# A new order of the mixer steps in a two-layer diffusion backbone, and modulation weights loaded in rows of 2 KB

## The chip, the cores and the metric

The kernel runs on one core of a Trainium2 chip. Its time is device microseconds of one execution; the median of three runs of the kernel before is 1035.23 us (1034.37 to 1036.27). The core has a tensor engine (PE in the rows, with its weight loads as PEld), a vector engine (DVE), a scalar engine (ACT), GpSimd (POOL) and SyncE (SP), which here issues most of the DMA transfers. Each engine works through its own list of instructions in order and waits where one of them needs another engine's result. The clock granted to PE has two levels here, 1.2 and 2.4 GHz; the profile shows it as PEclk, 0.5 and 1.0.

## The reference, cut to what matters

One inference step through two layers. 128 context tokens and 256 latent tokens, width 1024. Each layer modulates a normalised input by six vectors that come from a conditioning vector and a weight matrix (w_ada, 1024 x 6144), runs a token mixer and then a SwiGLU channel mixer:

```python
def adaln(cvec, w, b):
    mod = jnp.einsum('nd,de->ne', jax.nn.silu(cvec), w) + b
    return jnp.split(mod[:, None, :], 6, axis=-1)

def trunk_layer(x, mods, mixer_w, g_norm_l, w_gu_l, w_down_l, ctx):
    sh1, sc1, ga1, sh2, sc2, ga2 = mods
    h = modulate(rms_norm(x, g_norm_l[0]), sh1, sc1)
    mix, new_ctx = token_mixers(h, *mixer_w, ctx)
    x = x + ga1 * rms_norm(mix, g_norm_l[1])
    f = swiglu(modulate(rms_norm(x, g_norm_l[2]), sh2, sc2), w_gu_l, w_down_l)
    x = x + ga2 * rms_norm(f, g_norm_l[3])
    return x, new_ctx
```

The token mixer projects its input once (w_in), feeds three parallel groups of heads, and projects their joined outputs (w_out). A is neighbourhood attention with a relative bias (4 heads), B grouped-query attention with normalised and rotated queries and keys (8 query heads, 2 key heads), C a bidirectional mLSTM in chunks of 64 (4 heads), with gates, a running maximum, weighted scores, states from a cache and an output gate:

```python
    z = jnp.einsum('btd,de->bte', h, w_in_l)
    ...
    h_ml, fin_f, fin_b = mlstm_bidir(mq, mk, mv, mg, st_f0, st_b0)
    o_ml = mlstm_output(h_ml, mo, g_ml_l)
    mix = jnp.concatenate([merge_heads(o_na), merge_heads(o_gqa), o_ml], axis=-1)
    out = jnp.einsum('bte,ed->btd', mix, w_out_l)
```

All is float32. A product with weights is made of three matmuls on a high and a low part of each operand.

## The kernel before, in words

All 384 tokens stay in SBUF as three blocks of 128. A layer is a mixer, then a channel mixer (ffn). Weights stream from HBM by SP into the raw buffers (tag raw, three slots; line 126). Each is split into a high part by ACT (line 118) and a low part by DVE (line 119), and three matmuls use them (lines 108 to 110).

Inside a mixer the order of work on PE, DVE and ACT is written by hand: SCHEDULE holds one string of tokens for each layer, and step() runs them one after the other (line 1192 on). Each token's instructions join the lists of the three engines in that order; POOL and SP are not bound by it, and take their work as the framework orders it. The tokens that matter here:

- f: the next piece of projection work (71 in a layer): the input projection, first to the gates, then to tiles named tps (transposed results) or fps (features of queries and keys), later the first part of the output projection. A1 to A4 bring on the splits of weights ahead.
- t (layer 0 only): one of 12 chunks of 1 MB of w_ada, loaded into araw (two slots, line 167) and multiplied on PE (adap, line 219), added on DVE (acc, line 227). When a vector is complete, PE turns it (adat, line 237) and DVE makes Bmod (line 244), or it is spread over all partitions by POOL into G (line 210). In the channel mixer the other chunks are multiplied on DVE (line 177).
- s: the next small job of the norm and rotation of queries and keys.
- scans and rexp: the mLSTM's gates, with four kinds of scans on DVE (lines 800 to 813).
- L, E, C, U with a number 0 to 3: one unit of the mLSTM, a pair of heads in one direction. L loads the weights' rows into W by POOL (line 865) and masks them (line 868); E takes exponentials on ACT (line 885); C multiplies them by the scores S on DVE (line 909, or 894 and 895; units 0 and 2 also compute S on PE, line 907, for the unit that follows); U sums on PE (nd, lines 920 and 924) and divides on DVE (lines 929 to 939). W2 takes the buffer of the key weights kw, free after cout, and W3 that of W0, free after U0. S of the second pair takes the PSUM banks of the first.
- krow, kw, cin, cout, decay, cols: key weights (line 961), states in and out (line 968), decays.
- ogate: the output gate, two passes on ACT (lines 976 and 977) and a multiplication on DVE (line 978).
- hsum, hrstd, hnorm: the norm of the mLSTM's heads (line 1001 frees hml).
- bias, K0, K1: SP loads the relative bias, nb, in eight transfers (line 1088), the second four into the buffer that hml used; K0 and K1 transpose the cached keys on PE and mask the bias on DVE (line 1092).
- rT, rmix, kout: the mLSTM's outputs turned and joined; keys to the output.
- c, e, p, v with a number: one unit of attention: scores on PE (sc, line 1019), soft-max on ACT and DVE (nm, P, line 1033), its transposes (ptp, line 1048) and the products with the values.
- b, r, g, x, q, y and digits: the second part of the output projection, the norms and the residual.

The loop that runs the tokens is

```python
        for c in SCHEDULE[l].split():
            step(c)
```

Of the kernel before, what the change touches and what calls it, by code (L numbers as in the profile page):

```python
# [16 lines left out]
D = 1024  # L17
# [3 lines left out]
NEG = -1e30  # L21
SCHEDULE = (
    (
# [9 lines left out]
    ),  # L33
    (
# [8 lines left out]
    ),  # L43
)
ENGINES = {mybir.EngineType.PE, mybir.EngineType.DVE, mybir.EngineType.Activation}
# [7 lines left out]
def hybrid_step(  # L53
# [8 lines left out]
    V, A, PE, G, SP = nc.vector, nc.scalar, nc.tensor, nc.gpsimd, nc.sync  # L62
# [75 lines left out]
    def rstd_from(dst, ss, scale):  # L138
        A.activation(dst, ss, AF.Ln, bias=eps, scale=scale)
        A.activation(dst, dst, AF.Exp, scale=-0.5)  # L140

    Gt = {}

    class Ada:
# [14 lines left out]
        def issue(self, l, vec, kk):  # L159
            e0 = vec * D  # L160
            if kk == 0 and vec in (2, 5):
                for n, src in enumerate((b_ada[l, e0:e0 + D], g_norm[l, vec // 3 * 2 + 1])):
                    for r in range(4):
                        half = r // 2 * 512
                        G.dma_start(gbn[r:128:32, n], src[half:half + 512].rearrange("(g f) -> g f", g=4))
            raw = ap_.tile([128, 2, D], F32, tag="araw", name="araw", bufs=2)
            SP.dma_start(raw, w_ada[l, kk * 256:(kk + 1) * 256, e0:e0 + D].rearrange("(k p) f -> p k f", p=128))
            self.pend += [(l, vec, kk, raw, part) for part in range(self.parts)]

        def mul_v(self, l, vec, kk, raw, part):  # L170
# [35 lines left out]
        def spread(self):  # L206

            for l, n, row in self.rows:
                Gt[l, n] = ap_.tile([128, 2, D], F32, tag="G", name="G", bufs=1)
                G.dma_start(Gt[l, n], row.rearrange("s g f -> s (g f)").unsqueeze(0).broadcast_to([128, 2, D]))  # L210
            self.rows = []

        def mul_p(self, l, vec, kk, raw, part):
# [107 lines left out]
    def half_sum(n, h, ss):  # L321
# [4 lines left out]
        else:  # L326
            A.activation(ss[:, 0:1], ss[:, 1:2], AF.Ln, bias=ss[:, 2:3])
            A.activation(ss[:, 0:1], ss[:, 0:1], AF.Exp, scale=-0.5)

    HALVES = (slice(0, 512), slice(512, 1024))  # L330

    def post(i, halves, dst, g):
        rs = sumsq_rstd(halves)
        for n, h in enumerate(halves):
            V.tensor_tensor(dst[:, HALVES[n]], h, g[:, min(i, 1), HALVES[n]], ALU.mult)
        for h in HALVES:
            V.scalar_tensor_tensor(x[:, i, h], dst[:, h], rs, x[:, i, h], ALU.mult, ALU.add)

    def norm_x(i, t=None):
        rs = sumsq_rstd([x[:, i]])  # L340
        if t is None:
            t = tp.tile([128, D], F32, tag="t4", name="xn")
        for h in HALVES:
            V.tensor_scalar(t[:, h], x[:, i, h], rs, None, ALU.mult)
# [26 lines left out]
    def mixers(l, ma, mp, mn, pp, banks, h1T, steps, pairs, tails):  # L371
# [4 lines left out]
        def out_parts(ch, half):  # L376
            cs = HALVES[half]
            if ch in (0, 3):
                return w_parts(wl_out, 768 if ch == 0 else 0, 2, half * 512, 512)
            j0 = 2 * (ch - 1)  # L380

            def parts(raw):
                rv = raw.rearrange("p (k f) -> p k f", k=2)
                return [(rv[64 * w:64 * w + 64],
                         wl_out[256 + 256 * w + 64 * j0:256 + 256 * w + 64 * (j0 + 2), cs].rearrange(
                             "(j p) f -> p j f", p=64)) for w in range(2)]
            return parts
# [354 lines left out]
        def out_first():  # L742
            ps, w = {}, {}
            for half, ch, i in [(0, 0, i) for i in range(3)] + [
# [6 lines left out]
                if ch:  # L751
                    if not half:
                        oP.append(ma.tile([128, D], F32, tag="m4", name="oP", bufs=4))
                    A.activation(oP[i][:, HALVES[half]], ps[half, i], AF.Copy)
                yield

        def out_second(i):
            ps = [pp.tile([128, 512], F32, tag="w", name="ops2") for _ in range(2)]
            for ch in (1, 2):
                for half, h in enumerate(HALVES):  # L760
                    if i == 0:
# [644 lines left out]
    for l in range(DEPTH):  # L1406
        with tc.tile_pool(name="ma", bufs=1, reuse_waits="tile") as ma, \
                tc.tile_pool(name="mb", bufs=1, reuse_waits="tile") as mb, \
                tc.tile_pool(name="mn", bufs=1, reuse_waits="tile") as mn, \
                tc.tile_pool(name="p_w", bufs=1, space=PSUM, reuse_waits="tile") as p_w, \  # L1410
                ExitStack() as banks:
            pp = Pools({"w": p_w}, {"w": 3})
            pp.single(banks, 5)
            if l == 0:
                h1T, pairs, tails = new_hT(), [], []
            steps = [] if l else [(l, v) for v in (3, 2, 4)]
            if l == 0:
                cp1, cp2 = (pp.tile([128, 512], F32, tag="b", name=n) for n in ("cT", "cT2"))
                with tc.manual_schedule(engines={mybir.EngineType.PE}):
                    PE.transpose(cp1[:, 0:16], crow, ident[0:16, 0:16])  # L1420
                    PE.transpose(cp2[:, 64:128], grow, ident[0:64, 0:64])
                    PE.transpose(cp2[:, 128:224], brow, ident[0:96, 0:96])
                V.tensor_copy(scol[:, :, 2:4], cp1[:, 0:16].rearrange("p (s k) -> p k s", s=2))
                V.tensor_copy(gcol, cp2[:, 64:128].rearrange("p (l n k) -> p l n k", l=DEPTH, n=4))
                V.tensor_copy(bcol, cp2[:, 128:224].rearrange("p (l n k) -> p l n k", l=DEPTH, n=6))
            else:
                spread()
            h2 = mixers(l, ma, mb, mn, pp, banks, h1T, steps, pairs, tails)
# [65 lines left out]
```

## Time and profile before

| of the profiled execution | |
|---|---|
| its time | 1036.46 us |
| its span in the trace | 1034.7 us |
| PE busy | 971.1 us (94%) |
| DVE busy | 622.4 us (60%) |
| ACT busy | 466.3 us (45%) |
| POOL busy | 79.9 us (8%) |
| mean granted clock of PE | 0.969 |
| DMA | 167.21 MB, mean 162 GB/s |

The span runs from the first to the last instruction on the chip; the time holds 1.8 us more around it. Layer 0's mixer reaches to about 255 us and its channel mixer from there to about 523; layer 1's mixer lies from about 560 to 757, and its channel mixer behind it. A share of busy time is a mean over stages: in the channel mixers PE is never idle, and what idle time there is lies in the mixers. In rows of the timeline, the bracket at the end gives the time that the engine stood idle ahead of the instruction and the engine and line that ended it.

### The profile page before, as it was taken

The numbers are of one execution on the slowest core, as the hardware profiler recorded it, in microseconds if no ns is written. First come the engines' busy times: TensorE is split into PE (matmuls) and PEld (weight loads), VectorE is DVE, ScalarE is ACT, GpSimd is POOL, SyncE is SP. The second block draws the span as 40 slices with busy tenths as digits, with TensorE's granted clock in tenths as the row PEclk, the third lists the DMA queues.
The fourth block names the chain that finished last, engine by engine and source line by source line (L and its number), as shares of the span: only waits on it lengthen the run. The fifth ranks groups of instructions, "written<-read, shape, count | busy, mean of one in ns | idle before, by whom it ended". The sixth has DMA issues, their size and how long they took to land.

```text
span 1034.7 us, 15985 instructions
## 1 busy us (share of the span) xinstructions
PE 971.1 (94%) x6375; PEld 854.8 (83%) x6375; DVE 622.4 (60%) x940; ACT 466.3 (45%) x920; POOL 79.9 (8%) x138
## 2 busy tenths in 40 slices
PE   5999689799999999999999996989999999999997
PEld 3879587467999999999988785956699999999996
DVE  3557536567893798977556664476778533333324
ACT  3535514558833333333266454367883333333322
POOL 0302402000000200000210213000000001000000
PEclk9999869899999999999999997899999999999999
DMA  9958728611975587783334453331197434433001
GB/s 325 319 175 234 214 69 256 176 62 53 318 268 177 198 293 244 261 284 125 103 93 140 136 148 93 82 90 60 43 316 243 131 123 150 136 122 122 21 1 62
DMA packets 117052, 167.21 MB, mean 162 GB/s; under 512 B 14961, under 2 KB 89473, under 8 KB 116465
## 3 DMA queue, kind: packets, MB, share of 16 engines
q1 hardware_dynamic: 111328, 153.93, 46.6%
q0 software_dynamic: 5280, 12.10, 4.0%
q8 instruction: 50, 0.82, 0.3%
q14 instruction: 26, 0.21, 0.1%
q10 hardware_dynamic: 368, 0.16, 0.1%
HBM read 163.46 MB, written 2.70 MB: 161 GB/s over the span
## 4 chain that ended last, share of the span: by engine, by line
PE 72%; DVE 6%; ACT 5%; issue 3%; DMA 2%; POOL 0%; SPq 0%; DVEq 0%; ACTq 0%; POOLq 0%
PE gups L110 11%; PE gups L109 11%; PE gups L108 11%; PE facc L108 6%; PE facc L110 6%; PE facc L109 6%; ACT P L1033 2%; PE nd L924 2%; PE ptp L1048 1%; PE sc L1019 1%; PE tps L109 1%; PE tps L110 1%; PE tps L108 1%; PE ops L108 1%; DMA raw<-in_w_out_dram 1%
## 5 line engine op out<-in xcount | busy, mean ns | idle before, releaser
L119 DVE TENSOR_TENSOR lo<-raw,hi 128x1024 fp32r<-128x1024 f32 (+2 forms) x100 | 120.4, 1210 | 85.1 <-ACT hi L118 84.8
L118 ACT ACTIVATE hi<-raw 128x1024 fp32r<-128x1024 f32 (+2 forms) x100 | 103.7, 1042 | 106.8 <-PE facc L110 81.6
L110 PE MATMUL gups<-hT,ring 128*128 128x384 f32 x416 | 140.7, 338 | 0.0
L108 PE MATMUL gups<-hT,ring 128*128 128x384 f32 x416 | 140.7, 338 | 0.0
L109 PE MATMUL gups<-hT,ring 128*128 128x384 f32 x416 | 140.6, 338 | 0.0
L177 DVE SCALAR_TENSOR_TENSOR spare<-araw,scol,spare 128x1024 f32<-128x1024 f32 x98 | 120.7, 1277 | 2.3 <-DMA araw<-in_w_ada_dram 2.0
L108 PE MATMUL facc<-hi,f 128*128 128x512 f32 x240 | 95.6, 398 | 0.0
L109 PE MATMUL facc<-lo,f 128*128 128x512 f32 x240 | 94.7, 395 | 0.0
L110 PE MATMUL facc<-hi,f 128*128 128x512 f32 x240 | 94.7, 395 | 0.0
L109 PEld LDWEIGHTS gups<-hT,ring 128*128 128x128 f32 x416 | 78.2, 188 | 0.5
L108 PEld LDWEIGHTS gups<-hT,ring 128*128 128x128 f32 x416 | 78.1, 188 | 0.5
L110 PEld LDWEIGHTS gups<-hT,ring 128*128 128x128 f32 x416 | 78.1, 188 | 0.0
L108 PE MATMUL gups<-hT,xring 128*128 128x384 f32 x224 | 75.8, 338 | 0.0
L110 PE MATMUL gups<-hT,xring 128*128 128x384 f32 x224 | 75.8, 338 | 0.0
L109 PE MATMUL gups<-hT,xring 128*128 128x384 f32 x224 | 75.7, 338 | 0.0
L108 PE MATMUL tps<-hi,hT 128*128 128x512 f32 (+2 forms) x192 | 67.1, 349 | 2.2 <-DVE hT L509 2.2
L109 PE MATMUL tps<-lo,hT 128*128 128x512 f32 (+2 forms) x192 | 65.3, 340 | 3.4 <-DVE lo L119 3.4
L110 PE MATMUL tps<-hi,hT 128*128 128x512 f32 (+2 forms) x192 | 65.4, 341 | 0.0
L1226 ACT ACTIVATE ring<-rgu 128x1024 fp32r<-128x1024 f32 x26 | 27.6, 1062 | 68.2 <-PE gups L109 35.0
L1226 ACT ACTIVATE ring<-spare 128x1024 fp32r<-128x1024 f32 x26 | 27.5, 1059 | 62.4 <-PE gups L109 37.5
L108 PEld LDWEIGHTS facc<-hi,f 128*128 128x128 f32 x240 | 45.2, 188 | 10.8 <-issue 1.4
L110 PEld LDWEIGHTS facc<-hi,f 128*128 128x128 f32 x240 | 45.2, 188 | 10.5
(299 smaller groups left out, 1995.8 us busy)
## 6 DMA issues: line engine op xcount, KB each, us to landing
araw<-in_w_ada_dram SPq DMA_DIRECT2D x40, 1024.0 KB, 5.6
raw<-in_w_down_dram SPq DMA_DIRECT2D x44, 512.0 KB, 4.7
spare<-in_w_gu_dram SPq DMA_DIRECT2D x20, 1024.0 KB, 5.5
rgu<-in_w_gu_dram SPq DMA_DIRECT2D x20, 1024.0 KB, 5.1
raw<-in_w_in_dram SPq DMA_DIRECT2D x36, 512.0 KB, 5.2
sraw<-in_w_ada_dram SPq DMA_DIRECT2D x16, 512.0 KB, 9.3
raw<-in_w_out_dram SPq DMA_DIRECT2D x8, 512.0 KB, 5.9
raw<-in_w_out_dram SPq DMA_DIRECT2D x16, 256.0 KB, 5.2
```

Of the source, the lines that this page charges most:

```text
L108: PE.matmul(out, lhsT=wh, rhs=xh, start=start, stop=False)
L109: PE.matmul(out, lhsT=wh, rhs=xl, start=False, stop=False)
L110: PE.matmul(out, lhsT=wl, rhs=xh, start=False, stop=stop)
L118: a = A.activation(hi[:, :n], raw, AF.Copy)
L119: v = V.tensor_tensor(lo[:, :n], raw, hi[:, :n].bitcast(F32), ALU.subtract)
L177: V.scalar_tensor_tensor(acc[s], raw[:, part], scol[:, k, 2 + s:3 + s], acc[s], ALU.mult, ALU.add)
L924: PE.matmul(ndv[:, ti, hd], lhsT=W[:, hd, o:o + 128], rhs=vml[:, st, 2 * j + hd], start=ti == 0, stop=ti == 0 or (hd == 1 and n == len(ter ...
L1019: PE.matmul(sc[cc:cc + 64, hd, u * nk:(u + 1) * nk], lhsT=qT[pr, cc:cc + 64], rhs=kT[pr], start=True, stop=True)
L1033: A.activation(Pv[:, hd, u], self.sv[:, hd, u], AF.Exp, bias=nm[:, 0, hd, u:u + 1], accum_out=nm[:, 1, hd, u:u + 1])
L1048: PE.transpose(pt[:, hd, b * 128:(b + 1) * 128], self.P[:, hd, b * 128:(b + 1) * 128], ident)
L1226: A.activation(hi, rv, AF.Copy)
```

## The change

Both strings of SCHEDULE are written in a new order, with the same tokens. The w_ada chunk of 1 MB and the spread of G are each issued as two transfers of 512 KB, one for each half of the columns, so that a row of the w_ada transfer has 2 KB in place of 4 KB. The diff, with one line of each string:

```diff
@@ SCHEDULE, layer 0, the first line of the string
-        "f f f f f f f f f gates scans f f f t f f f f f f f t f s f s rexp L0 s f s f f f s f f Q0 s f s f f f s "
...
+        "f f f f f f f f f f f gates f f t f f f f f f f f scans s s rexp f f s L0 f s f t f f f f f f s Q0 f s "
...
@@ SCHEDULE, layer 1, where units 0 to 2 stand
-        "f s Q1 f s f f Q2 f f f krow f s cols kw decay cin L1 f f E0 C0 s cout L2 E1 s ogate C1 f f U0 L3 s s s "
...
+        "f s f Q1 s f f Q2 f f f krow f cols decay kw f cin E0 L1 f cout C0 L2 s ogate L3 s E1 f C1 s s E2 U0 s "
...
@@ class Ada
+    HALVES = (slice(0, 512), slice(512, 1024))
...
             raw = ap_.tile([128, 2, D], F32, tag="araw", name="araw", bufs=2)
-            SP.dma_start(raw, w_ada[l, kk * 256:(kk + 1) * 256, e0:e0 + D].rearrange("(k p) f -> p k f", p=128))
+            for h in HALVES:
+                SP.dma_start(raw[:, :, h], w_ada[l, kk * 256:(kk + 1) * 256, e0 + h.start:e0 + h.stop].rearrange(
+                    "(k p) f -> p k f", p=128))
...
                 Gt[l, n] = ap_.tile([128, 2, D], F32, tag="G", name="G", bufs=1)
-                G.dma_start(Gt[l, n], row.rearrange("s g f -> s (g f)").unsqueeze(0).broadcast_to([128, 2, D]))
+                for n2, h in enumerate(HALVES):
+                    G.dma_start(Gt[l, n][:, :, h], row[:, 4 * n2:4 * n2 + 4].rearrange("s g f -> s (g f)").unsqueeze(0)
+                                .broadcast_to([128, 2, 512]))
```

The rows below show the lists of single engines at three places, before and then after; lines of the changed kernel are one to four higher or lower than those of the kernel before.

First place: DVE in layer 0, from the gates (gt) to the scans (R). Before:

```order
L712 TENSOR_TENSOR gt<-tps,bg 128x2x4 x6
L783 SCALAR_TENSOR_TENSOR R<-R_707 64x384
L786 SCALAR_TENSOR_TENSOR R_707<-R_707,R 64x384
L800 SCALAR_TENSOR_TENSOR R<-ones,R_707 32x128
L800 SCALAR_TENSOR_TENSOR R<-ones,R_707 32x256
```

And after:

```order
L714 TENSOR_TENSOR gt<-tps,bg 128x2x4 x6
L118 TENSOR_TENSOR lo<-raw,hi 128x1024
L785 SCALAR_TENSOR_TENSOR R<-R_728 64x384
L788 SCALAR_TENSOR_TENSOR R_728<-R_728,R 64x384
L118 TENSOR_TENSOR lo<-raw,hi 128x1024 x3
L802 SCALAR_TENSOR_TENSOR R<-ones,R_728 32x128
L802 SCALAR_TENSOR_TENSOR R<-ones,R_728 32x256
```

Four splits of weights (lo), which stood behind the scans, now stand ahead of them, one ahead of the gates' sums and three behind these.

Second place: PE in layer 0, from the scores of the second pair of heads through units 1 and 2 (nd; a unit is five rows of nd, and two units that meet share a row). Before:

```order
L907 MATMUL S_1375<-qTm,kTm 64x128 x4
L237 MATMUL adat<-cst,acc 128x128
L219 MATMUL adap<-araw,scol 32x128 x16
L924 MATMUL nd<-share,W 128x65 x2
L920 MATMUL nd<-CT,decq 128x130
L924 MATMUL nd<-share,W 128x65 x4
L920 MATMUL nd<-CT,decq 128x130
L924 MATMUL nd<-share,W 128x65 x4
L920 MATMUL nd<-CT,decq 128x130
L924 MATMUL nd<-share,W 128x65 x2
L920 MATMUL nd<-CT,decq 128x130
L924 MATMUL nd<-share,W 128x65 x4
```

And after, from the last projection matmuls between units 1 and 2 to the first behind unit 2:

```order
L108 MATMUL tps<-lo,hT_125 128x256
L109 MATMUL tps<-hi,hT_126 128x256
L241 MATMUL adat<-cst,acc 128x128
L223 MATMUL adap<-araw,scol 32x128 x16
L926 MATMUL nd<-share,W 128x65 x2
L922 MATMUL nd<-CT,decq 128x130
L926 MATMUL nd<-share,W 128x65 x2
L922 MATMUL nd<-CT,decq 128x130
L926 MATMUL nd<-share,W 128x65 x4
L107 MATMUL fps<-hT_125,hi 128x384
L108 MATMUL fps<-hT_126,hi 128x384
L109 MATMUL fps<-hT_125,lo 128x384
```

Before, units 1 and 2 followed each other and adat and adap came ahead of unit 1; now unit 1 follows the scores at once, twelve matmuls of projection (tps), adat and adap come between the two units, and twelve more of projection (fps) between units 2 and 3.

Third place: ACT in layer 1, from the state output (Cout) to the exponentials of the second unit (W), with the two passes of the output gate (share). Before:

```order
L970 ACTIVATE Cout<-cop 65x512
L885 ACTIVATE W<-W,share 128x128 x2
L885 ACTIVATE W<-W,share 128x256
L885 ACTIVATE W<-W,share 128x128 x2
L885 ACTIVATE W<-W,share 128x256
L139 ACTIVATE s_5786<-s_5786,eps 128x2
L140 ACTIVATE s_5786<-s_5786 128x2
L976 ACTIVATE share<-share,ones 128x768
L977 ACTIVATE share<-share 128x768
```

And after:

```order
L972 ACTIVATE Cout<-cop 65x512
L640 ACTIVATE t_5838<-z 128x128
L978 ACTIVATE share<-share,ones 128x768
L979 ACTIVATE share<-share 128x768
L138 ACTIVATE s_5840<-s_5840,eps 128x2
L139 ACTIVATE s_5840<-s_5840 128x2
L887 ACTIVATE W<-W,share 128x128 x2
L887 ACTIVATE W<-W,share 128x256
L887 ACTIVATE W<-W,share 128x128 x2
L887 ACTIVATE W<-W,share 128x256
```

The output gate's two passes now stand ahead of the second unit's exponentials, where they stood behind them.

## Rows read from the trace of the kernel before

**Rows 1.** Table of stretches: start:end, length, busy us (count) by engine, PEclk, DMA share, GB/s

```profile
108.86:147.10 38.24, 27.52 (x236) 24.95 (x236) 16.13 (x44) 11.36 (x31) 9.55 (x14) 0.64 0.38 122
168.90:197.75 28.85, 22.36 (x230) 15.09 (x230) 18.85 (x29) 15.76 (x45) 1.36 (x2) 1.00 0.97 255
255.00:523.00 268.00, 268.00 (x1601) 249.37 (x1600) 206.67 (x224) 106.27 (x147) 13.75 (x25) 1.00 0.66 224
613.88:655.70 41.82, 30.52 (x224) 28.53 (x224) 21.18 (x49) 15.21 (x44) 10.55 (x14) 0.71 0.35 94
638.70:642.10 3.40, 2.33 (x22) 2.33 (x21) 2.36 (x7) 0.84 (x4) 0.00 (x0) 1.00 0.00 0
642.10:655.70 13.60, 10.63 (x41) 10.05 (x40) 7.14 (x18) 3.72 (x8) 0.00 (x0) 0.50 0.12 39
```

**Rows 2.** Timeline, PE: start, us, engine, line, [idle before <- what ended it]

```profile
67.88 0.50 PE L109 MATMUL tps<-lo,hT 128*128 128x512 f32 x1 [1.68 <-DVE lo L119]
...
106.55 1.06 PE L968 MATMUL cop<-kw,share 128*65 128x128 f32 x8 [1.50 <-DVE kw L961]
...
582.81 0.50 PE L109 MATMUL tps<-lo,hT 128*128 128x512 f32 x1 [1.68 <-DVE lo L119]
```

**Rows 3.** Timeline, PE, layer 0, mLSTM units

```profile
112.95 0.63 PE L924 MATMUL nd<-share,W 128*128 128x65 f32 x4 [0.46 <-issue]
...
114.37 1.00 PE L924 MATMUL nd<-share,W 128*128 128x65 f32 x8
118.15 1.32 PE L907 MATMUL S<-qTm,kTm 64*64 64x128 f32 x32 [2.78 <-DVE W L894]
...
123.36 1.94 PE L219 MATMUL adap<-araw,scol 128*32 128x128 f32 x32 [2.66 <-DVE Bmod L244]
```

**Rows 4.** Timeline, layer 0, DVE and then ACT around the second unit

```profile
116.27 0.96 DVE L978 TENSOR_TENSOR share<-share,gml 128x768 f32<-128x768 f32 x1 [1.08 <-ACT share L977]
117.14 0.95 DVE L894 TENSOR_TENSOR W<-W,S 128x768 f32<-128x768 f32 x1
118.01 0.41 DVE L895 TENSOR_TENSOR W<-W,S 128x256 f32<-128x256 f32 x1
...
122.72 2.08 ACT L885 ACTIVATE W<-W,share 128x128 f32<-128x128 f32 x6 [1.85 <-POOL W L868]
```

**Rows 5.** Timeline, layer 1, DVE and then PE, mLSTM units

```profile
628.46 0.96 DVE L978 TENSOR_TENSOR share<-share,gml 128x768 f32<-128x768 f32 x1 [6.53 <-ACT share L977]
...
631.85 1.08 PE L924 MATMUL nd<-share,W 128*128 128x65 f32 x4 [6.54 <-DVE hml L935]
...
639.77 0.66 PE L924 MATMUL nd<-share,W 128*128 128x65 f32 x4 [1.07 <-DVE W L909]
```

**Rows 6.** Timeline, bias tiles: SP's loads, DVE's masks, layers 0 and 1

```profile
157.35 2.61 SPq L1088 DMA_DIRECT2D nb<-in_na_bias_dram  x4
...
169.02 0.56 DVE L1092 TENSOR_TENSOR nb<-nb,cst 128x384 f32<-128x384 f32 x1 [2.79 <-DMA nb<-in_na_bias_dram]
...
661.88 2.61 SPq L1088 DMA_DIRECT2D nb<-in_na_bias_dram  x4
...
670.29 0.56 DVE L1092 TENSOR_TENSOR nb<-nb,cst 128x384 f32<-128x384 f32 x1 [0.75 <-DMA nb<-in_na_bias_dram]
```

**Rows 7.** Timeline, PE and ACT: scores behind soft-max

```profile
200.06 1.56 PE L1019 MATMUL sc<-kTn,qTn 64*64 64x384 f32 x8 [6.80 <-ACT P L1033]
...
197.83 1.06 ACT L118 ACTIVATE hi<-raw 128x1024 fp32r<-128x1024 f32 x1 [6.28 <-DMA raw<-in_w_out_dram]
...
674.54 1.10 PE L1019 MATMUL sc<-share 64*64 64x128 f32 x32 [1.24 <-ACT P L1033]
```

**Rows 8.** DMA issues: what, queue, count, KB each, median us to landing

```profile
araw<-in_w_ada_dram SPq DMA_DIRECT2D x40, 1024.0 KB, 5.6
raw<-in_w_down_dram SPq DMA_DIRECT2D x44, 512.0 KB, 4.7
...
rgu<-in_w_gu_dram SPq DMA_DIRECT2D x20, 1024.0 KB, 5.1
```

More of the change, by code (lines that the diff above doesn't have):

```diff
@@ L328, in half_sum @@
             A.activation(ss[:, 0:1], ss[:, 0:1], AF.Exp, scale=-0.5)
-    HALVES = (slice(0, 512), slice(512, 1024))
     def post(i, halves, dst, g):
```

30 rows, old and new, of the table SCHEDULE are left out of this document.

## The prediction, made before the changed kernel ran

> **What bounds the kernel now.** I read the page's slices first, then the table of stretches, then the timeline of the tensor engine with what ended each idle time. In the slices PE is busy nearly throughout, and it dips, with PEclk, only in the mixers of the two layers. The stretch of the first channel mixer has PE busy 268.00 of 268.00 us at clock 1.00 [rows 1]: an order of mixer steps can win nothing there. So I price the change in the mixers alone, as (a) PE idle time and (b) PE work done at 1.2 GHz in place of 2.4.
>
> Two stretches hold most of both [rows 1]. Layer 0, from the end of the first score matmuls to 147.10: 38.24 us, PE busy 27.52, idle 10.72, mean clock 0.64. Layer 1, from 613.88 to 655.70: 41.82 us, busy 30.52, idle 11.30, clock 0.71. Rescaled to 2.4 GHz by durations that the trace has at that level (one step U of the mLSTM sums 2.42 us, from 112.95 to 115.37 [rows 3]; twice that when slow), the work in them is about 18.5 and 23.25 us. So the slow clock costs 27.5 - 18.5 = 9.0 us in layer 0 and 30.5 - 23.25 = 7.3 us in layer 1.
>
> **The change part by part.** No step is removed or added; the sum is of idle time and clock.
>
> a) Scans. In both layers PE stands 1.68 us behind a weight split on DVE [rows 2], because the four gate scans and what belongs to them stand in front of that split in DVE's order. Now four splits stand before the scans (order of the change, first place). Saved 2 x 1.68 = 3.4; if the splits are instead late for want of raw data, as little as 0. I take 3.4: what DVE does with the scans later stands beside two more pieces of projection.
>
> b) The state output waited 1.50 us for the key weights on DVE [rows 2]; these now stand two pieces of projection earlier. Saved 1.5 (0 to 1.5); it lies ahead of the stretch of c.
>
> c) Layer 0, mLSTM units. What stops PE there before: the second unit's weighted scores stand on DVE behind the output gate's multiplication (0.96), which waited for ACT [rows 4], so PE stood 2.78 us before the next S; then 2.66 us before the modulation matmuls behind Bmod [rows 3], besides smaller ones. Now the gate's ACT work comes before the second exponentials, and projection pieces (one of tps, some 1.6 us by the timeline, and two of fps, 1.04 each) stand between U1, U2 and U3. Walk from the end of S at 0: two modulation matmuls 2.2, U0 to 4.6, S to 5.9; DVE has C1 ready at about 6.6 (ACT: the gate's two passes, about 0.9 each, and exponentials of 2.08; DVE: 0.96, then 0.95 + 0.41 [rows 4]), so PE idles 0.7; U1 to 9.0, projection to 10.6, adat and adap to 11.9, U2 to 14.3, projection to 16.4. Unit 3's weights take U0's buffer. Before, its exponentials could begin 7.35 us after U0's end (122.72 [rows 4] less 115.37) and took 2.08, so C3 (1.36 on DVE) is ready at about 4.6 + 7.35 + 2.08 + 1.36 = 15.4 and U3 does not wait. The walk thus leaves 0.7 us idle; because the path acc to adat to Bmod to adap is still there, which cost 2.66, I take 3.5. Idle falls from 10.7 to 3.5 (7.2). Of the 9.0 of slow clock I leave 4 standing (two U at half speed, 2 x 2.1). Gain 7.2 + 5.0 = 12.2; ends: 0.7 when the clock stays down, 19 when neither is left.
>
> d) Layer 1, mLSTM units. The 6.54 us before U1 [rows 5] is DVE: the gate's multiplication waited 6.53 us, since ACT did the second exponentials (waiting for their weights) before the gate, and U0's own division stands behind both on DVE. Now the gate is ahead of these exponentials on ACT (third place of the order) and a projection piece covers part. What is late next: the second pair's S waits for the PSUM banks that C1 frees, about 2.1; U1 0.75 and U2 1.35 behind DVE. That is 4.2 idle in place of 11.3; of the 7.3 of slow clock I leave 5 (two slow U plus). Gain 7.1 + 2.3 = 9.4; ends -5.7 and 18.
>
> e) Past keys. In layer 0, K1 now comes before K0 and two or three projection pieces after the bias loads. Its mask waits on DVE for the second bias tile, whose buffer is free only after the normalised heads. In layer 1 before, those four loads went out at 661.88 and the last was masked at 670.29, 8.4 us later [rows 6]; with K1 moved up, DVE stands still there, and behind it the hT copies and splits. Three projection pieces and the rest hide all but some 1.6 of it, 5.4 if loads land as late as in layer 0 (157.35 to 169.02). I take -1.6 (range -5.4 to 0). In layer 1, K1 comes ahead of the first soft-max, whose reciprocal then stands behind the mask: PE's wait there was 1.24 [rows 7], I expect 3.3, so -2.1 (0 to -5).
>
> f) Output weights, layer 0. PE stood 6.80 us before scores, since ACT, in order, was held 6.28 us by a split whose raw data had not landed [rows 7]. From the last bias tile's landing (168.9) to there the DMA engines were 0.97 busy at 255 GB/s [rows 1]: 7.4 MB, a limit of transfer and not of order. By the new order I count half a MB more ahead of that split, so 31 us at the same rate. PE came to its wait 24.3 us after that landing (193.26 - 168.9). Now K1 stands earlier, so that three more projection pieces (1.04 each) and the transposes of rT and K0 come between, together about 4: 28.4 us. The wait is then 31 - 28.4 = 2.6, so +4.2 (0 to 6.8).
>
> g) The modulation weights. One load of 1024 KB took 5.6 us, a load of 512 KB 4.7 [rows 8]. Two halves one after the other would be 9.4, two side by side 4.7: so -3.8 to +0.9 a load. The w_gu loads of 1024 KB come in rows of 1 KB and took 5.1 us, no longer than those of 4 KB rows; and where DMA is the limit the loads overlap on the queue. I take 0. The same for G. The issues on SP (about 0.4 to 0.6 us each) are hidden while SP waits for buffers.
>
> Sum: 3.4 + 1.5 + 12.2 + 9.4 - 1.6 - 2.1 + 4.2 = 27.0. The profiled execution took 1036.5 (span 1034.7), 1.2 over the median of the runs, 1035.2. So 1036.5 - 27.0 = 1009.5, and by the median 1008.3. I predict 1008.5.
>
> The Trainium skill, page "TensorE: Matmul & The Clock Gate", section "HAM oscillation — how this bites in real kernels", says that idle gaps of the tensor engine throw it back to the half clock. By it, an order with no long gap would keep 2.4 GHz and my charges of 4 and 5 would go: about 999. The trace speaks against leaning on it: the clock fell at 642.10 though the 3.40 us before it had PE busy 2.33 with no gap over 1.07 [rows 1, 5]. So I keep the charges.
>
> **Rivals.**
> 1. The clock stays low (the slower side). If it falls before U0 and does not come back between the units, as at 642.10 where it stayed at 0.50 for 13.6 us at PE busy 10.63 [rows 1], layer 0 takes 37.5 us (gain 0.7) and layer 1 about 47.5 (loss 5.7). With 3.4 + 1.5 - 1.6 - 2.1, and f at 0 because the raw data then waits as before: -3.8, so 1039. For it: small gaps remain around each U. Against: the added projection pieces are dense work. It decides the sign from the point where the slow clock costs 31.8 us in the two stretches (my charge of 9 and what is left of the gain without f, 22.8); here that is 15.5 + 20.
> 2. The halves cost transfer time. Five loads of 1 MB (four of modulation weights, one G) lie in the stretch of 0.97 DMA share in layer 0; at +3.8 each 19 us: 1028. The skill's page "DMA: Bandwidth & Descriptors", section "Rules for kernel authors", asks for at least 1 MiB per DMA, which speaks for it; the 5.1 us of the 1 KB rows [rows 8] against it.
> 3. The waits of e at their far ends (3.8 + 2.9 more), f at 0 (4.2): 1019.
> 4. PE's waits only move: the units are bound by ACT, DVE and the reload of W, so c and d give nothing, and f is 0. Left are 3.4 + 1.5 - 1.6 - 2.1 = 1.2: 1034. For it: each unit is a chain over four engines; against: the longest waits there are behind work that the chain doesn't need (the output gate, Bmod).
> 5. No clock charge and f whole: 1008.5 - 9 - 2.6 = 997.
>
> **How the numbers follow.** Forecast 0.53 (1002 to 1016), rival 1 0.08, rival 2 0.10, rival 3 0.15, rival 4 0.06, rival 5 0.08. What a measurement can tell here is 0.2%, 2 us. Faster: 0.53 + 0.10 + 0.15 + 0.08, 0.86; same 0.05 (most of rival 4); slower 0.09 (rival 1 and a rest of rival 4). The range of 996 to 1030 takes in the forecast, rivals 2, 3 and 5 with some of their spread cut off, and leaves out rivals 1 and 4: some 0.82 inside.
>
> **What would show it.** Right: no PE gap behind a split near 66 and 581; the layer 0 stretch near 26 us and the layer 1 stretch near 32, each with a clock over 0.8; no gap over 2.5 us before a U; the wait before scores near 195 under 4 us; the w_ada halves landing together. Wrong: the same stretches at clock 0.5 to 0.6, DVE idle at the mask for over 4 us with PE waiting, a PE wait over 7 us behind raw data in layer 0, or any change in the channel mixers' 535 us.

## The result, and the profile after

The changed kernel took 1018.7 us (median of 4 runs, 1013.69 to 1022.54) against 1035.13 of the kernel before (1034.37 to 1036.27): ratio 0.9851, 95% interval 0.9815 to 0.9887, so 15.4 us faster (11.7 to 19.1). The forecast was 1008.5, in a range of 996 to 1030. The direction was right and the time lies in the range, but outside the 1002 to 1016 that the prediction gives to its forecast itself, and the forecast gain of 26.7 us is 1.7 times the measured one. The changed kernel's runs differ by up to 9 us. The profiled run is the fastest of the four, 1013.69, so its trace shows 22.8 us of gain, more than the median run has; the experiments tell what of it is the change's.

The table of stretches of the changed kernel, columns as in [rows 1]:

```profile
104.34:127.02 22.68, 17.91 (x234) 16.22 (x235) 13.14 (x33) 9.46 (x26) 8.57 (x13) 1.00 0.73 231
148.20:181.00 32.80, 29.40 (x323) 21.70 (x323) 20.83 (x34) 18.75 (x51) 6.79 (x11) 0.96 0.90 247
...
234.31:504.00 269.69, 269.69 (x1610) 251.10 (x1609) 206.75 (x223) 107.77 (x148) 14.98 (x26) 1.00 0.66 223
590.93:624.76 33.83, 27.71 (x223) 26.26 (x222) 17.51 (x42) 16.96 (x46) 11.11 (x15) 0.80 0.44 109
605.00:618.60 13.60, 11.08 (x59) 10.55 (x51) 8.08 (x25) 6.11 (x19) 2.78 (x4) 0.50 0.22 50
717.70:728.00 10.30, 4.84 (x22) 4.56 (x22) 7.76 (x14) 6.23 (x18) 0.00 (x0) 0.67 0.98 335
```

The first row answers to layer 0's units in [rows 1] (there 38.24 us and clock 0.64, of which the last 3.1 us lie behind unit 3; here 22.68 to the end of unit 3 and clock 1.00): idle 4.77, no slow clock. The second runs from the transposes of K0 to the wait for raw output weights, with a DMA share of 0.90. The channel mixer, third, is PE-bound as before. The fourth row is layer 1's units, from the state transposes (ctp) to the end of unit 3: PE idle 6.12, and 13.60 us of it, the fifth, still at 1.2 GHz. The last row is new: at the end of layer 1's mixer, where the kernel before waited 0.90 us at most, PE is busy 4.84 of 10.30 us at clock 0.67.

PE in layer 0's units, and then what it waits for later in the layer (K0's transposes, scores):

```profile
106.44 1.08 PE L223 MATMUL adap<-araw,scol 128*32 128x128 f32 x32 [1.09 <-DVE acc L231]
110.33 1.32 PE L909 MATMUL S<-qTm,kTm 64*64 64x128 f32 x32
111.77 0.63 PE L926 MATMUL nd<-share,W 128*128 128x65 f32 x4
...
116.13 1.08 PE L223 MATMUL adap<-araw,scol 128*32 128x128 f32 x32 [0.29 <-DVE Bmod L248]
...
124.61 0.63 PE L926 MATMUL nd<-share,W 128*128 128x65 f32 x4 [2.35 <-DVE hml L937]
...
148.19 0.47 PE L687 MATMUL tT<-cst,kcn 128*128 128x128 f32 x1 [4.79 <-DVE acc L231]
...
182.14 1.56 PE L1021 MATMUL sc<-kTn,qTn 64*64 64x384 f32 x8 [3.56 <-ACT P L1035]
```

What answers to [rows 3]: S and U1 (110.33, 111.77) now follow U0 without a wait, where S had waited 2.78; adap waits 0.29 for Bmod in place of 2.66; and 2.35 are left before U3. 4.79 before the transposes of K0 and 3.56 before scores (6.80 in [rows 7]) are the waits of terms e and f. DVE and ACT at these two:

```profile
144.61 0.56 DVE L1094 TENSOR_TENSOR nb<-nb,cst 128x384 f32<-128x384 f32 x1 [6.64 <-DMA nb<-in_na_bias_dram]
147.38 0.56 DVE L1094 TENSOR_TENSOR nb<-nb,cst 128x384 f32<-128x384 f32 x1 [2.21 <-DMA nb<-in_na_bias_dram]
...
179.74 1.06 ACT L117 ACTIVATE hi<-raw 128x1024 fp32r<-128x1024 f32 x1 [4.34 <-DMA raw<-in_w_out_dram]
```

DVE stood 6.64 and 2.21 us at K1's mask for the second bias tile (2.79 in [rows 6]), and the sum acc on which PE waits stands behind it; ACT stood 4.34 us for raw output weights. In layer 1, DVE and PE at K1's mask, which now comes ahead of the first soft-max (PE waited 1.24 there in [rows 7]):

```profile
640.62 0.56 DVE L1094 TENSOR_TENSOR nb<-nb,cst 128x384 f32<-128x384 f32 x1 [3.94 <-DMA nb<-in_na_bias_dram]
...
644.89 1.10 PE L1021 MATMUL sc<-share 64*64 64x128 f32 x32 [3.98 <-ACT P L1035]
```

In layer 1's units, POOL, ACT, DVE and PE at the second pair's scores:

```profile
591.64 1.44 POOL L867 DMA_DIRECT2D W<-mrow  x2 [14.07 <-PE ctp L948]
...
599.46 0.86 POOL L870 TENSOR_SCALAR_AFFINE_SELECT W<-W 128x768 f32<-128x768 f32 x1 [4.31 <-DMA W<-mrow]
...
600.36 0.69 ACT L887 ACTIVATE W<-W,share 128x128 f32<-128x128 f32 x2 [3.31 <-POOL W L870]
...
602.91 0.95 DVE L896 TENSOR_TENSOR W<-W,S 128x768 f32<-128x768 f32 x1 [5.47 <-ACT W L887]
...
604.01 1.52 PE L909 MATMUL S<-qTm,kTm 64*64 64x128 f32 x32 [3.56 <-DVE W L896]
606.15 1.09 PE L926 MATMUL nd<-share,W 128*128 128x65 f32 x4 [0.62 <-DVE hml L937]
...
612.57 1.08 PE L926 MATMUL nd<-share,W 128*128 128x65 f32 x4 [1.90 <-ACT s L138]
```

POOL could issue the second unit's weights W only when the state transposes (ctp) had ended; they were masked at 599.46, exponentiated from 600.36, multiplied at 602.91, and so S, which needs the banks that this frees, waited 3.56 us. [rows 5] had 6.54 at the place of U1. Last, PE at the end of layer 1's mixer, with DVE ahead of it:

```profile
721.17 1.41 DVE L1187 SCALAR_TENSOR_TENSOR x<-oP,ss,x 128x512 f32<-128x512 f32 x2
722.52 0.43 DVE L363 CAST hT<-xm 128x512 fp32r<-128x512 f32 x1
...
723.09 0.55 PE L107 MATMUL gu<-hT,hi 128*128 128x256 f32 x1 [5.38 <-DVE hT L363]
```

The channel mixer's first matmuls wait 5.38 us for hT, the first half of the second of the three blocks (step 01: the first digit is the half, the second the block, both counted from 0), which stands on DVE behind the last block's residual (x).

### The profile page after: what moved, and what is told of

It is laid out like the page before. It is cut to its first block, busy times and chain, and to the rows that moved or that the text cites. A ratio compares the mean times of both kernels' runs of the same rounds, so it can differ in the third digit from the quotient of the medians.

```text
span 1011.9 us, 16033 instructions
## 1 busy us (share of the span) xinstructions
PE 960.1 (95%) x6375; PEld 847.8 (84%) x6375; DVE 620.7 (61%) x940; ACT 466.3 (46%) x920; POOL 83.4 (8%) x142
## 5 line engine op out<-in xcount | busy, mean ns | idle before, releaser
L117 ACT ACTIVATE hi<-raw 128x1024 fp32r<-128x1024 f32 (+2 forms) x100 | 103.8, 1041 | 97.1 <-PE facc L109 80.3
```

What stands on the lines that cost most here:

```text
L117: a = A.activation(hi[:, :n], raw, AF.Copy)
```

## The experiments

Each was timed in 5 rounds beside the kernel before, whose medians were 1032.6 to 1033.8 there; a ratio times that is given in us. "Front" of a mixer is the time from the end of the last transposes ahead of its projection to the end of U3, "back" from there to the first matmul of the channel mixer, both from PE's timeline. Each kernel has one trace. A difference of two kernels by their ratios has an interval too, estimated here from the two intervals. Line numbers in these kernels are up to one higher than in the changed kernel.

**Which part gives the gain: four crosses.** The edits put one of the two strings, or the two loads, back (behind L0 the old string of layer 0 runs `s f f f f s f f Q0`; the line of it that is shown in the section on the change has an s for one of these f):

```diff
 layer0_new:  SCHEDULE = (new layer 0, old layer 1), loads in halves
 layer1_new:  SCHEDULE = (old layer 0, new layer 1), loads in halves
 halves_only: SCHEDULE = (old layer 0, old layer 1), loads in halves
 order_only:  SCHEDULE = (new layer 0, new layer 1), loads of 1 MB
```

layer0_new: 

> New order in layer 0 alone, with the halved loads; layer 1 as before. Theory (the gain is layer 0's order): layer 0's mixer took 214.8 us before and 194.1 after, so about 20 us are gained, 1013 to 1017. Rival 1 (both layers gain about alike, as the prediction's 18 and 9): 1017 to 1022. Rival 2 (a run's clock decides, not the order): anywhere between 1013 and 1030, with a spread of over 5 us between runs.

layer1_new: 

> New order in layer 1 alone, with the halved loads; layer 0 as before. Theory (layer 1's new order nets almost nothing, 3.8 us in the mixer less 2.4 at the slow clock at the start of its channel mixer): 1032 to 1036. Rival 1 (layer 1 gains 9): 1024 to 1028. Rival 2 (the clock decides): spread of over 5 us between runs.

halves_only: 

> Both old orders, only the loads of the modulation weights and the spread of G in halves. Theory (a half costs nothing): 1033 to 1037. Rival (halves cost transfer time where DMA is the limit, up to 3.8 us for each of five loads): up to 1054. Rival (halves help, since matmuls on the first half or the wait for raw data end sooner): 1028 to 1032.

order_only: 

> Both new orders, loads of 1 MB as before. Theory (a half costs and gives nothing): 1014 to 1022, as the changed kernel. Rival (halves cost): 1000 to 1012. Rival (halves help): 1024 or more.

| kernel | median us | ratio (95%) | gain us |
|---|---|---|---|
| layer0_new | 1016.51 | 0.9854 (0.9826 to 0.9883) | 15.1 |
| layer1_new | 1032.49 | 1.0000 (0.9983 to 1.0017) | 0.0 |
| halves_only | 1031.95 | 0.9995 (0.9978 to 1.0012) | 0.5 |
| order_only | 1015.69 | 0.9842 (0.9821 to 0.9862) | 16.3 |

As far as the intervals tell, layer 0's order is the whole gain; layer 1's new order gives nothing, and the halves neither cost nor give. The theory's 20 us for layer 0 was too much: it was read from one trace on each side. The spread of over 5 us that rival 2 named did come, 9.0 us in layer0_new, but the interval is clear of it. The time of halves_only, 1031.95, lies in the range of the rival that halves help; by the ratio to the kernel before, which took 1032.57 in the same rounds, they do not. The DMA issues of halves_only show a half and what it replaces in [rows 8]:

```profile
araw<-in_w_ada_dram SPq DMA_DIRECT2D x80, 512.0 KB, 5.0
```

The two halves of a load go out 0.42 us apart, and by the 21 pairs of that trace that have both landings the second is there 6.6 us (median) after the first went out, where one load of 1 MB took 5.6. So a load comes about 1 us later, and no time is lost by it that a measurement shows. The Trainium skill, page "DMA: Bandwidth & Descriptors", section "Rules for kernel authors", asks for 1 MiB or more per DMA for the highest bandwidth. Here half of that made no difference in time (0.9995, 0.9978 to 1.0012).

**Where in layer 0: front or back.**

```diff
 front0: layer 0 new through U3, then
+ "hsum s s f s s f s t f s s kT f s s f hrstd t f hnorm f t rT bias f f K0 f f t rmix f A2 s K1 ..." (the old rest)
 back0:  layer 0 old through U3, then
+ "f s f s f t s f f f hsum hrstd f s hnorm f f bias t f A1 A2 f K1 f A2 A2 f t rT K0 f rmix ..." (the new rest)
```

front0: 

> In layer 0 the new order as far as the last mLSTM sum U3, then the old order (head norm, bias, K0 before K1, attention), made to fit by moving the small jobs; layer 1 old; halved loads. Theory (the mLSTM front of layer 0 gives the gain, by idle time and by the clock that no longer falls there; the back part gives little because the raw output weights are limited by transfer): 14 to 19 us under the kernel before. Rival (front and back give half each): 7 to 12 us under it.

back0: 

> The other cross: in layer 0 the old order as far as U3, then the new one (K1 ahead of K0, attention); layer 1 old; halved loads. Theory: within 4 us of the kernel before, since what K1 costs (4.8 us of idle time in the changed kernel) and what the raw wait gives cancel. Rival: 7 to 12 us under it.

front0 took 1017.85 us, 0.9848 (0.9830 to 0.9866), a gain of 15.7; back0 1034.47, 1.0008 (0.9991 to 1.0025), a loss of 0.8. The front alone is the gain, as far as the intervals tell. Scores behind the raw output weights, PE, in halves_only, in layer1_new and in back0:

```profile
193.88 0.88 PE L1022 MATMUL sc<-kTn,qTn 64*64 64x384 f32 x8 [1.59 <-ACT P L1036]
```

```profile
197.13 1.56 PE L1022 MATMUL sc<-kTn,qTn 64*64 64x384 f32 x8 [5.06 <-ACT P L1036]
```

```profile
168.32 0.47 PE L688 MATMUL tT<-cst,kcn 128*128 128x128 f32 x1 [6.09 <-DVE acc L232]
...
202.11 0.88 PE L1022 MATMUL sc<-kTn,qTn 64*64 64x384 f32 x8 [2.83 <-ACT P L1036]
```

halves_only and layer1_new have the same old order in layer 0, and the wait is 1.59 in one and 5.06 in the other, 6.80 in the kernel before. With the new back it is 2.83, and 6.09 are lost ahead of it at K0's transposes, which stand behind K1's mask. Over all traces the back took 104.1 to 111.8 us with the old order of it and 105.1 to 111.5 with the new one (units0_bare, below, left out, which has three pieces more there). That fits the limit by transfer that the prediction named, by which what one wait gives the other takes; no run shows that limit by itself. That the order of the back has no effect that can be measured is shown by the two ratios.

**Why the front gains: two steps undone in the changed kernel.**

```diff
 gate0_back, layer 0
- cout C0 s s t ogate t s s E1 L3 s s C1
+ cout C0 s s t t s s E1 L3 s s ogate C1
 units0_bare, layer 0
- U1 s f t E3 t C3 U2 f f U3 s f s
+ U1 s t E3 t C3 U2 U3 f f f s f s
```

gate0_back: 

> The changed kernel with the output gate of layer 0 put back behind the second exponentials, one step. Theory (the gate's place held the second unit's scores before): DVE's gate multiplication waits for two ACT passes of 0.9 behind E1, so C1 and U1 come 2 to 3 us later, and the clock falls in the units; layer 0's front (first projection to end of U3, 86.8 us in the changed kernel) becomes 90 to 97. Rival (the projection pieces alone did it): front within 1 us of 86.8.

units0_bare: 

> The changed kernel with the three projection pieces that stand between units 1, 2 and 3 of layer 0 put behind unit 3. Theory (they fill PE's waits, and by that keep its clock up): the time is 4 us longer by the idle time alone, with 1.2 GHz over the units some 10 us longer; in the trace PE idle between U1 and U3 of 4 us or more, and a stretch of over 10 us at 1.2 GHz there. Rival 1 (idle time alone): 3 to 4 us, clock as in the changed kernel. Rival 2 (the units wait anyway): no change.

units0_bare took 1024.57 us, 0.9907 (0.9892 to 0.9921): 5.8 us (1.8 to 9.8) more than the changed kernel by the ratios. Its stretches, from the first score matmuls to the end of U3 and the part at 1.2 GHz (columns as in [rows 1]), and PE ahead of the fall:

```profile
105.34:130.64 25.30, 19.59 (x211) 17.59 (x211) 12.01 (x32) 7.87 (x22) 8.57 (x13) 0.73 0.69 209
116.80:133.90 17.10, 14.67 (x88) 13.73 (x89) 4.88 (x14) 2.63 (x9) 3.17 (x5) 0.50 0.33 90
```

```profile
107.45 1.08 PE L224 MATMUL adap<-araw,scol 128*32 128x128 f32 x32 [1.09 <-DVE acc L232]
...
116.85 0.45 PE L242 MATMUL adat<-cst,acc 128*128 128x128 f32 x1 [1.66 <-DVE ht L941]
...
126.12 1.09 PE L927 MATMUL nd<-share,W 128*128 128x65 f32 x4 [1.65 <-DVE hml L938]
```

The stretch holds three projection pieces less (3.7 us) than the first row of the changed kernel, and is 2.6 us longer. PE idle in it is 5.71 against 4.77, so idle time explains 0.9; the clock explains the rest: it was at 0.50 for 17.1 us, in which PE was busy 14.67. Between U1 and U3 PE is idle for 4.04, as expected. So the pieces act by keeping the engine at 2.4 GHz more than by filling waits. This sets the slowest run of units0_bare beside the fastest of the changed kernel; but all runs point the same way, with a median granted clock of 0.968 in the five of units0_bare, 0.977 in the four of the changed kernel and 0.975 in the six of gate0_back. The clock fell with no wait over 1.66 ahead of it, and in the changed kernel it stayed up behind the wait of 2.35. The Trainium skill, page "TensorE: Matmul & The Clock Gate", section "HAM oscillation — how this bites in real kernels", describes a fall behind long idle gaps. Here the longest single wait does not tell where it falls.

gate0_back took 1018.89, 0.9860 (0.9837 to 0.9883), 0.9 us (-3.5 to 5.3) more than the changed kernel, which is within the noise. Its trace shows the step's mechanism, DVE and then PE:

```profile
110.67 0.96 DVE L981 TENSOR_TENSOR share<-share,gml 128x768 f32<-128x768 f32 x1 [1.45 <-ACT share L980]
111.54 0.95 DVE L897 TENSOR_TENSOR W<-W,S 128x768 f32<-128x768 f32 x1
...
112.54 1.32 PE L910 MATMUL S<-qTm,kTm 64*64 64x128 f32 x32 [1.93 <-DVE W L897]
```

The gate's multiplication waits for ACT and S waits 1.93 us that it does not in the changed kernel, as expected; the wait of 2.35 before U3 is gone for it, so that PE idle in the front is no longer than in the other kernels. The clock fell in the units too, as expected: it was at 1.2 GHz for 6.8 us from 113.73, earlier than in any trace with the gate ahead but best, below (108.7 there). But the price is too small to tell by the time, and the front of 89.1 us is no proof, since fronts of the same new order took 86.5 to 89.2. Expectation half met: the wait and the fall are there, but this step is not most of the gain.

All traces side by side say more than one pair. Layer 0's front is split here into PE idle, half of PE's busy time at 1.2 GHz (an estimate of what the slow clock costs, since a unit took 2.42 us at 2.4 GHz in [rows 3] and 4.51 at 1.2 in units0_bare, from 119.96 to 124.47) and the rest:

| traces | front us | idle | slow clock | rest |
|---|---|---|---|---|
| old order of the front: before, halves_only, layer1_new, back0 | 103.0 | 12.9 to 13.9 | 8.5 to 9.7 | 80.3 to 80.5 |
| new: changed, layer0_new, order_only, front0, and tail1, tail1_k, cin1_early below | 86.5 to 89.2 | 4.2 to 5.2 | 0 to 2.3 | 81.8 to 82.0 |
| gate0_back | 89.1 | 4.4 | 3.4 | 81.3 |
| units0_bare | 90.1 | 6.3 | 5.7 | 78.0 |

The rest is the same within 0.3 us in each group, so the split holds. The new front gains some 8 to 10 us of idle time and 6 to 10 of slow clock, and pays 1.5 for the two pieces more that stand in it. Without the three pieces 1.1 to 2.1 of the idle time and 3.4 to 5.7 of the slow clock are back.

**Why layer 1 gives nothing: three repairs.**

```diff
 tail1, layer 1
- v13 A2 b2 A1 A3 11 b2 r2a g2a r2b g2b x2a x2b 01 A1 q2a
+ v13 A2 b2 01 A1 A3 11 b2 r2a g2a r2b g2b x2a x2b A1 q2a
 tail1_k = tail1 and, in layer 1
- rmix K1 f f f c0 f e0 kout c1 K0 p0 f A2 f A2
+ rmix f f f c0 f e0 kout c1 K0 p0 f A2 K1 f A2
 cin1_early = tail1_k and, in layer 1
- Q1 s f f Q2 f f f krow f cols decay kw f cin E0 L1 f cout
+ Q1 s cin L1 f f Q2 f f f krow f cols decay kw f E0 f cout
```

tail1: 

> The changed kernel with one step of layer 1 moved back: the transposes of the first block's second half (01) ahead of the last block's norm. Theory (the 5.38 us before the channel mixer's first matmuls and the slow clock behind it come from this step, which stands behind the last block's norm on ACT and DVE): 5 to 8 us under the changed kernel, ratio to the kernel before 0.977 to 0.981. Rival (PE would wait there for weights or for the last block anyway): ratio as the changed kernel, 0.984 to 0.986.

tail1_k: 

> As the kernel before in this list, and in layer 1 K1 (mask of the second bias tile) behind the first soft-max, two pieces of projection behind K0. Theory (DVE waits 3.94 us at the mask for the bias loads while the first soft-max stands behind it, and PE loses 3.98 us and some of its clock): another 3 to 6 us, ratio 0.972 to 0.977. Rival (the wait only moves to the next soft-max): no change against the kernel before it in the list.

cin1_early: 

> The kernel with both repairs (the step 01 and K1 in layer 1), and in layer 1 the state transposes and the load of the second unit's weights (cin, L1) some 9 us earlier, ahead of Q2. Theory (the second unit's weights take the buffer that the state transposes read, so C1 came 12 us after these whatever stood between; that is the 3 to 4 us wait before the second S, and the clock falls behind it): the wait goes, layer 1's front of 90.6 becomes 79 to 84, ratio to the kernel before 0.965 to 0.971. Rival (the next weights, for units 2 and 3, are late just as well and the clock still falls): front 88 to 90.6, ratio 0.975 to 0.978.

| kernel | median us | ratio (95%) | layer 1 front, back, channel mixer (its trace) |
|---|---|---|---|
| before | 1035.13 | 1 | 95.8, 96.5, 280.3 |
| changed | 1018.70 | 0.9851 | 90.1, 98.3, 282.7 |
| tail1 | 1012.99 | 0.9805 (0.9784 to 0.9825) | 90.8, 94.7, 280.3 |
| tail1_k | 1010.62 | 0.9772 (0.9753 to 0.9791) | 90.6, 92.8, 280.3 |
| cin1_early | 1003.71 | 0.9715 (0.9690 to 0.9740) | 87.0, 92.8, 280.3 |

The last column reads the answer: the new front of layer 1 gained 5.7 us, with three projection pieces more in it; its back lost 1.8 with three pieces less, and the channel mixer lost 2.4 at the slow clock. With step 01 moved ahead of the last block's norm, PE passes to the channel mixer without a wait (no bracket, where the changed kernel had 5.38; 1.04 are left ahead of the transposes two us before):

```profile
726.78 0.28 PE L108 MATMUL gu<-hT,hi 128*128 128x256 f32 x1
```

So PE did not wait for weights or the last block there, as the rival had it. The theory for tail1 held, at the lower edge of what was expected (4.8 us less by the ratios, 0.5 to 9.0), and so did that for tail1_k (3.4 less, 0.5 to 6.3). With the first soft-max ahead of the mask, PE's wait there is 1.04 in place of 3.98:

```profile
647.84 1.10 PE L1022 MATMUL sc<-share 64*64 64x128 f32 x32 [1.04 <-ACT P L1036]
```

For cin1_early the wait before S went as expected, and the next one took part of it, as the rival said:

```profile
603.14 1.32 PE L910 MATMUL S<-qTm,kTm 64*64 64x128 f32 x32
605.34 0.63 PE L927 MATMUL nd<-share,W 128*128 128x65 f32 x4 [0.88 <-DVE hml L938]
...
611.11 0.97 PE L927 MATMUL nd<-share,W 128*128 128x65 f32 x4 [3.35 <-DVE ht L941]
```

S follows at once; U2 now waits 3.35 us for unit 1's division on DVE, which stands behind C2 there. The front became 87.0, not the 79 to 84 expected, and the ratio just missed its range; 5.9 us by the ratios (2.6 to 9.1) are nevertheless gained.

**Both repaired further.**

```diff
 best = cin1_early and, in layer 0 and in layer 1
- C3 U2 f f U3 s f s s f s s t
+ C3 U2 f f f f U3 s s s s s t
- E3 U1 s s s s U2 s f s C3 ... kT f f U3 f f f s s f bias
+ E3 U1 s s s s f f U2 s f s C3 ... kT f f U3 f s s f bias
```

> The kernel with the repairs and cin early, and two more projection pieces between the units where PE still waited: in layer 0 between units 2 and 3 (wait 2.33), in layer 1 between units 1 and 2 (wait 3.35), taken from behind unit 3. Theory (a piece put into a wait is free, and the clock stays up): 2.3 in layer 0 only if the raw output weights behind it, limited by transfer, do not take it back; 3 to 5 in layer 1; ratio 0.964 to 0.969. Rival (the pieces are then missing behind unit 3 and the wait moves to the head norm or the bias mask): ratio 0.970 to 0.974.

It took 1000.23 us (997.10 to 1002.19), 0.9678 (0.9655 to 0.9702), in the expected range: 33 us under the kernel before, 18 under the changed one and 3.8 (0.3 to 7.4) under cin1_early by the ratios. Its units, layer 0 and layer 1:

```profile
104.53:129.73 25.20, 22.90 (x246) 20.96 (x245) 13.15 (x33) 9.95 (x27) 9.55 (x14) 0.86 0.73 226
588.70:621.33 32.63, 28.94 (x270) 27.15 (x269) 20.46 (x44) 19.40 (x49) 8.87 (x13) 1.00 0.52 122
```

Layer 1's units now run at clock 1.00, PE busy 28.94 of 32.63 us. In layer 0 idle is down to 2.30, but the clock fell in this execution (0.86).

## Why the prediction was right, and too large

Measured parts beside the terms of the sum, from kernels that hold one part each:

| terms | forecast us | measured us (95%) | kernel |
|---|---|---|---|
| a, b, c in layer 0 (front) | 1.7 + 1.5 + 12.2 = 15.4 | 15.7 (13.9 to 17.6) | front0 |
| e, f in layer 0 (back) | -1.6 + 4.2 = 2.6 | -0.8 (-2.6 to 0.9) | back0 |
| a, d, e in layer 1 | 1.7 + 9.4 - 2.1 = 9.0 | 0.0 (-1.8 to 1.8) | layer1_new |
| g, halves | 0 | 0.5 (-1.2 to 2.3) | halves_only |
| sum | 27.0 | 15.4 (11.7 to 19.1) | the changed kernel |

The first three kernels hold the halved loads too, so that the fourth row is not to be added to theirs.

- a, b, c: the mechanism right, the sum right in part by luck. No wait of 1.68 behind a split is left in either layer, and the 1.50 before the state output is gone. Idle in the units was put at 3.5 and is 4.77; slow clock at 4 and is 0 in this trace (0 to 2.3 in others of the same order). The slow clock of [rows 1] cost 10.1 by half of PE's busy time at 1.2 GHz (8.5 of it up to U3), where the prediction had 9.0. So idle time gave less than forecast (9.2 in the whole front of layer 0, against 10.4), the clock more (8.5 against 5.0), and the two pieces more in the front, some 1.5, are in no term; these three nearly cancel. That the pieces between the units matter is shown; that the gate's step alone matters is not.
- e in layer 0 was mis-sized: 1.6 forecast, 4.79 measured, inside its bound of 5.4. f was put at 2.6 of wait and is 3.56 here, 1.26 to 5.65 in the other traces with the new back. Its failing step is that e and f were priced apart: together they were to give 2.6 and gave nothing (-0.8, -2.6 to 0.9). That what K1 loses and what the raw wait gives are the same time, in a stretch limited by transfer, fits the traces and is argued. Rival 3 (e at its far end in both layers, f nothing) comes to 1019, the measured time, but by luck: for layer 0 it has -5.4 where -0.8 was measured, and it lacks what the end of layer 1 cost.
- d, layer 1: idle 6.12 where 4.2 was forecast, of it 3.56 before S (2.1 forecast, a number for which the prediction names no row); slow clock 13.60 us with PE busy 11.08, so 5.5 lost (5 forecast). Against the prediction's 11.3 and 7.3 for the kernel before that is 7.0 where 9.4 was forecast. Mechanism right, the term too large: the prediction saw that S needs C1 but not that C1's weights wait for the state transposes.
- The failing step is what the prediction left out: the end of layer 1's mixer, the order of the last norm and transposes, was not priced at all. It cost 5.38 us of idle time and 2.4 of slow clock in the channel mixer, where the prediction saw that an order can win nothing, but not that it can lose. With the mask in layer 1 (3.98 where 3.3 was forecast, and slow clock behind it) it gives back what layer 1's front gained; tail1 and tail1_k show both.
- Of the prediction's own signs of being wrong two came: DVE stood over 4 us at the mask with PE waiting (6.64), and a channel mixer changed (282.7 in place of 280.3). Of its signs of being right, the layer 0 and layer 1 stretches (22.68 and 33.83), no gap over 2.5 before a U and the wait of 3.56 before scores came; layer 1's clock of 0.80 is on the edge, and the halves landed 1.3 us apart in halves_only.
- Rival 1 (slow clock in both stretches) did not come true; rival 2 (dear halves) is refuted by halves_only; rival 4 (waits only move) has layer 1's nil in sum but not for its reason, since layer 1's front did gain 5.7, and is wrong for layer 0's front; rival 5 (no clock charge, f whole) is right of the units of layer 0 in this trace alone.

What stays open: how much of layer 0's gain each step of its front carries beyond the three pieces, which are 5.8 of the 15.7; and what decides, from one execution to the next, where the clock falls. A later K1 in layer 0 was not tried; the ratios of front0 and layer0_new, which differ in that among other steps of the back, are the same.

## What to carry to other kernels

Price a new order to its very end: a step put behind others that do not need it delays the next stage where that stage's first instruction reads it (5.38 us here). Where small dependent matmuls wait on other engines, put dense work between them, because the clock that it keeps up can be worth more than the wait that it fills (here 3.4 to 5.7 us against 1.1 to 2.1). And do not add up two waits in one stretch where the DMA engines are nearly always busy (0.97 in [rows 1]): here the sum of the two terms was 2.6 and nothing came of it.

## What was not expected of the hardware

Executions of one program differ by up to 9.4 us without any change (cin1_early, 999.37 to 1008.75). What makes the difference is not shown, since each kernel has one trace; but two things differ between kernels with the same order at the place: the wait for raw output weights in layer 0 was 1.59, 5.06 and 6.80 us in three of them, and the clock fell at other places: with layer 1's old order PE was at 1.2 GHz for 10.2 and 13.6 us around its units in the kernel before and for 27.3 without a break in layer0_new.
